# A column mean: one piece of the second-last slab split by rows, fewer loads for the last slab, and a filler matmul taken out

## The chip, the cores and the metric

The kernel runs on one core of a Trainium2 chip. The metric is the device time of one execution in microseconds (us). The engines are called PE (matmuls), PEld (PE's weight loads), DVE (vector), ACT (scalar), POOL and SP (which issues loads and stores here). Loads and stores are carried by 16 DMA engines.

## The reference

```python
def setup_inputs():
    return {"x": np.random.randn(8192, 8192).astype(np.float32)}

def reference(x: np.ndarray) -> np.ndarray:
    return np.mean(x, axis=0)
```

The input is 268 MB of float32; the output is one row of 8192 means.

## The kernel before

**Slabs and pairs.** The 8192 rows are 64 slabs of 128 rows, one row per partition, with all 8192 columns (32 KB a row). The first 62 slabs are read as 31 pairs, each into one of three rotating buffers named `pair` that hold two slabs side by side. Line 96 issues these loads on SP. The first pair comes in two loads, of 2048 columns and the rest; pairs up to the 28th in one load of 16384 columns, and the last three in two loads of 8192. On DVE, line 85 adds the running sum of the pair before to the left half of the new pair, and then the right half to the left half: two additions of 128 x 8192 for each pair. For the last pair the second addition is cut into four of 2048 columns (`parts`, line 107).

**The tail.** The last two slabs share one buffer, `tail`. Its left half is `slab` (slab 62), loaded at line 109 in two loads of 4096 columns. Its right half is `last` (slab 63), loaded at line 112 in nine loads whose widths are in `PIECES`: 2048, 2048, 2048, 1024, 256, 256, 256, 160 and 96 columns. All are issued by SP and served in the order of issue. SP issues a load only when the load eight places ahead of it has landed; the first tail load also waits until DVE has released its buffer.

**Sums over partitions.** PE multiplies by a matrix of ones (128 x 32), which sums the 128 partitions of each column into PSUM. `WIDE` gives four wide ranges of 2048, 2048, 2048 and 1024 columns: `fold_wide` issues four matmuls for a range, each into its own 32 rows of the range's PSUM bank. `NARROW` gives four narrow ranges of 256 columns, one matmul each in `fold_narrow`. A matmul on float32 data is two instructions in the profile. Each column gets three contributions: the running sum (`before`), slab 62 (`slab`) and slab 63 (`last`). For the last 2048 columns, which are wide range 3 and the narrow ranges, DVE adds slab 62 to the running sum first (line 119), so that two contributions are left.

**The order on PE** is the order in which the program is written, each instruction waiting for its data:
1. wide ranges 0, 1 and 2 on `before` and `slab`;
2. `close(0)`: wide range 0 on `last`, then ACT scales it by 1/8192 into `rw`;
3. the filler, line 135: one matmul of 512 columns of `slab` into the bank of narrow range 0, whose result is overwritten (`WARM` counts such matmuls);
4. `close(1)`;
5. wide range 3 and the four narrow ranges on `before`, which wait for DVE's last addition;
6. `close(2)` and `close(3)`;
7. the narrow ranges on `last`, range 3 in two matmuls of 160 and 96 columns. After each range DVE (ranges 0 and 2) or ACT (1 and 3) scales it into `row`.

**Stores.** POOL stores `rw` (line 143) when the third wide range is scaled; SP stores `r3` (line 147) and at the end `row` (line 159).

Of the kernel before, what the change touches and what calls it, by code (L numbers as in the profile page):

```python
# [1 line left out]

# [4 lines left out]

F32 = mybir.dt.float32
ADD = mybir.AluOpType.add
GROUPS = 4  # L10

WIDE = (2048, 2048, 2048, 1024)
NARROW = (256, 256, 256, 256)
PIECES = (2048, 2048, 2048, 1024, 256, 256, 256, 160, 96)
FIRST = 2048
BY_ROW = 3
WARM = 1


@with_exitstack
def kernel(
    ctx: ExitStack,
    tc: tile.TileContext,
    x: bass.AP,
    out: bass.AP,
):
    nc = tc.nc
    P = nc.NUM_PARTITIONS  # L30
    R, C = x.shape
    n_slabs = R // P
    n_pairs = n_slabs // 2 - 1
    N0 = sum(WIDE)
    assert n_slabs % 2 == 0 and n_pairs >= 4 and N0 + sum(NARROW) == sum(PIECES) == C
    inv_r = 1.0 / float(R)

    const_pool = ctx.enter_context(tc.tile_pool(name="const", bufs=1))
    pair_pool = ctx.enter_context(tc.tile_pool(name="pair", bufs=3))
    psum_pool = ctx.enter_context(  # L40
        tc.tile_pool(name="acc", bufs=1, space=bass.MemoryType.PSUM)
    )
    res_pool = ctx.enter_context(tc.tile_pool(name="res", bufs=1))


    ctx.enter_context(tc.manual_schedule())

    ones = const_pool.tile([P, 32], F32)
    nc.gpsimd.memset(ones, 1.0)  # L49

    wide, lo = [], 0
    for n, w in enumerate(WIDE):
        bank = psum_pool.tile([P, w // GROUPS], F32, name=f"wide{n}", tag=f"wide{n}")
        wide.append((lo, w, bank))
        lo += w
    narrow = []
    for n, w in enumerate(NARROW):
        bank = psum_pool.tile([P, 512], F32, name=f"narrow{n}", tag=f"narrow{n}")
        narrow.append((lo, w, 32 * n, bank))
        lo += w  # L60

    def mm(dst, src, **flags):
        nc.tensor.matmul(out=dst, lhsT=ones, rhs=src, skip_group_check=True, **flags)  # L63

    def fold_wide(n, src, **flags):
        lo, w, bank = wide[n]
        q = w // GROUPS
        for g in range(GROUPS):
            a = lo + g * q
            mm(bank[32 * g : 32 * g + 32, :], src[:, a : a + q], **flags)  # L70

    def fold_narrow(n, src, lo, hi, **flags):
        at, _, g, bank = narrow[n]
        mm(bank[g : g + 32, lo - at : hi - at], src[:, lo:hi], **flags)

    def scaled(dst, src, eng):
        if eng == "act":
            nc.scalar.mul(out=dst, in_=src, mul=inv_r)  # L78
        else:
            nc.vector.tensor_scalar(  # L80
                out=dst, in0=src, scalar1=inv_r, scalar2=None, op0=mybir.AluOpType.mult
            )

    def add(dst, a, b):
        nc.vector.tensor_tensor(out=dst, in0=a, in1=b, op=ADD)  # L85

    before = None
    for k in range(n_pairs):  # L90
        pair = pair_pool.tile([P, 2 * C], F32, tag="pair")
        src = x[2 * P * k : 2 * P * (k + 1), :].rearrange("(p j) c -> p (j c)", j=2)
        cut = FIRST if k == 0 else C if k >= n_pairs - BY_ROW else 2 * C
        for lo, hi in ((0, cut), (cut, 2 * C)):
            if lo < hi:
                nc.sync.dma_start(out=pair[:, lo:hi], in_=src[:, lo:hi])  # L96
        if before is not None:
            add(pair[:, 0:C], pair[:, 0:C], before[:, 0:C])
        if k < n_pairs - 1:
            add(pair[:, 0:C], pair[:, 0:C], pair[:, C : 2 * C])  # L100
        before = pair


    tail = pair_pool.tile([P, 2 * C], F32, tag="pair")
    r = (n_slabs - 2) * P
    slab, last = tail[:, 0:C], tail[:, C : 2 * C]
    parts = [(lo, lo + w) for lo, w, _ in wide[:3]] + [(wide[3][0], C)]
    for lo, hi in ((0, C // 2), (C // 2, C)):
        nc.sync.dma_start(out=slab[:, lo:hi], in_=x[r : r + P, lo:hi])  # L109
    lo = 0  # L110
    for w in PIECES:
        nc.sync.dma_start(out=last[:, lo : lo + w], in_=x[r + P : R, lo : lo + w])  # L112
        lo += w


    for lo, hi in parts:
        add(before[:, lo:hi], before[:, lo:hi], before[:, C + lo : C + hi])
    lo, hi = parts[3]
    add(before[:, lo:hi], before[:, lo:hi], slab[:, lo:hi])

    rw = res_pool.tile([P, 3 * 512], F32, name="rw")
    r3 = res_pool.tile([P, WIDE[3] // GROUPS], F32, name="r3")
    row = res_pool.tile([1, C - N0], F32, name="row")

    def close(n):
        fold_wide(n, last, start=False, stop=True)
        scaled(rw[:, n * 512 : (n + 1) * 512] if n < 3 else r3, wide[n][2], "act")

    for n in range(3):
        fold_wide(n, before, start=True, stop=False)  # L130
        fold_wide(n, slab, start=False, stop=False)
    close(0)

    for n in range(WARM):
        mm(narrow[0][3][0:32, :], slab[:, 0:512], start=True, stop=True)
    close(1)
    fold_wide(3, before, start=True, stop=False)
    for n, (lo, w, _, _) in enumerate(narrow):
        fold_narrow(n, before, lo, lo + w, start=True, stop=False)
    for n in range(2, 4):  # L140
        close(n)
    W3 = 3 * GROUPS * 512
    nc.gpsimd.dma_start(  # L143
        out=out[0:W3].rearrange("(n g w) -> g n w", g=GROUPS, w=512),
        in_=rw.rearrange("(g r) (n w) -> g r n w", r=32, w=512)[:, 0],
    )
    nc.sync.dma_start(
        out=out[W3:N0].rearrange("(g w) -> g w", g=GROUPS),
        in_=r3.rearrange("(g r) w -> g r w", r=32)[:, 0],
    )  # L150
    for n, (lo, w, g, bank) in enumerate(narrow):
        if n < 3:
            fold_narrow(n, last, lo, lo + w, start=False, stop=True)
        else:
            cut = C - PIECES[-1]
            fold_narrow(n, last, lo, cut, start=False, stop=True)
            fold_narrow(n, last, cut, C, start=False, stop=True)
        scaled(row[0:1, lo - N0 : lo - N0 + w], bank[g : g + 1, 0:w], "act" if n % 2 else "dve")
    nc.sync.dma_start(out=out[N0:C], in_=row)


# [1 line left out]
_INS = ['x']  # L163
_OUTS = [((8192,), 'float32')]


# [23 lines left out]
```

## Time and profile before

| what | value |
|---|---|
| time, median of 3 runs | 628.18 us (628.05 to 628.44) |
| the profiled execution's own time | 628.08 us |
| its span, first to last instruction | 626.3 us |
| DVE busy | 533.5 us (85%) |
| PE busy | 13.8 us (2%) |
| share of the span of 16 DMA engines, load queue | 99.3% |
| read from memory | 268.44 MB, 429 GB/s over the span |
| chain that ended last | DMA 73%, DVE 25% |
| first matmul, last matmul's start | 608.9 us, 623.4 us |

All times inside an execution are counted from the start of its span. A profile describes one execution; the time around its span (here 1.8 us) is not in it. In the chain that ended last, each step is followed back to what released it. In a table of stretches each row has a stretch's start and end, its length, the busy time of each engine with the number of instructions, the granted TensorE clock, the mean share of the DMA engines that were busy (1.00 is all sixteen), and GB/s. The trace also has a record of each DMA packet with its start, size, duration and queue, but not the engine that carried it.

### The profile page before, as it was taken

What the parts mean: (1) busy time and instruction counts of PE and PEld (TensorE: products, weight loads), DVE (VectorE), ACT (ScalarE), POOL (GpSimd) and SP (SyncE); (2) the same over time, 40 slices, a digit from 0 to 9 for tenths busy, and PEclk for the clock granted to TensorE, in tenths of its full rate; (3) what the DMA queues carried; (4) which work ended last, traced back from release to release, by engine and by line L of the source; (5) the groups of instructions that cost most, each with busy time, mean ns of one, the idle gap of its engine ahead of it and who ended that gap; (6) DMA issues with size and microseconds to landing.
All of it is one profiled execution on the core that took longest, in us unless ns stands there. A gap on an engine that the chain in (4) does not pass through costs nothing.

```text
span 626.3 us, 454 instructions
## 1 busy us (share of the span) xinstructions
PE 13.8 (2%) x108; PEld 4.3 (1%) x108; DVE 533.5 (85%) x67; ACT 4.2 (1%) x7; POOL 1.0 (0%) x6
## 2 busy tenths in 40 slices
PE   0000000000000000000000000000000000000017
PEld 0000000000000000000000000000000000000002
DVE  0538988889888899888898888988889888899995
ACT  0000000000000000000000000000000000000001
POOL 0000000000000000000000000000000000000000
PEclk9999999999999999999999999999999999999999
DMA  9999999999999999999999999999999999999997
GB/s 415 401 456 402 469 402 469 402 469 402 452 419 435 435 419 452 402 469 402 469 402 469 402 469 402 469 402 465 406 465 406 465 406 465 402 431 435 427 422 302
DMA packets 6685, 268.50 MB, mean 429 GB/s; under 512 B 909, under 2 KB 1425, under 8 KB 1562
## 3 DMA queue, kind: packets, MB, share of 16 engines
q1 hardware_dynamic: 6634, 268.45, 99.3%
q0 software_dynamic: 48, 0.02, 0.0%
q8 instruction: 1, 0.02, 0.0%
q14 instruction: 2, 0.02, 0.0%
HBM read 268.44 MB, written 0.03 MB: 429 GB/s over the span
## 4 chain that ended last, share of the span: by engine, by line
DMA 73%; DVE 25%; SPq 0%; PE 0%; issue 0%; ACT 0%; DVEq 0%
DMA pair<-in_x_dram 69%; DVE pair L85 25%; DMA tail<-in_x_dram 5%; SPq L112 0%; PE narrow L63 0%; SPq L96 0%; SPq L109 0%; PE wide L63 0%; ACT row L78 0%; DVEq L85 0%
## 5 line engine op out<-in xcount | busy, mean ns | idle before, releaser
L85 DVE TENSOR_TENSOR pair<-pair 128x8192 f32<-128x8192 f32 (+1 forms) x64 | 530.4, 8292 | 84.9 <-DMA pair<-in_x_dram 83.8
L63 PE MATMUL wide<-pair,ones 128*32 128x512 f32 (+1 forms) x32 | 4.9, 681 | 608.9 <-DVE pair L85 608.9
L63 PE MATMUL wide<-tail,ones 128*32 128x512 f32 (+1 forms) x56 | 7.7, 634 | 0.9 <-DMA tail<-in_x_dram 0.9
L78 ACT ACTIVATE rw<-wide 128x512 f32<-128x512 f32 x3 | 1.8, 597 | 618.4 <-PE wide L63 618.4
L63 PEld LDWEIGHTS wide<-pair,ones 128*32 128x32 f32 x32 | 1.2, 135 | 611.3 <-issue 610.7
L80 DVE TENSOR_SCALAR row<-narrow 1x256 f32<-1x256 f32 x2 | 0.8, 415 | 5.4 <-PE narrow L63 5.4
L63 PE MATMUL narrow<-tail,ones 128*32 128x256 f32 (+3 forms) x12 | 2.5, 385 | 0.0
L85 DVE TENSOR_TENSOR pair<-pair,tail 128x2048 f32<-128x2048 f32 x1 | 2.3, 2291 | 0.0
L63 PEld LDWEIGHTS wide<-tail,ones 128*32 128x32 f32 x56 | 1.7, 118 | 6.4 <-DMA tail<-in_x_dram 3.6
L143 POOL DMA_DIRECT2D out_dram<-rw x1 | 0.7, 695 | 621.7 <-ACT rw L78 621.7
L78 ACT ACT_TABLE_LOAD x1 | 1.3, 1283 | 0.7 <-PEq L174 0.7
L63 PEld LDWEIGHTS narrow<-tail,ones 128*32 128x32 f32 x12 | 1.1, 108 | 1.3 <-issue 0.6
L78 ACT ACTIVATE row<-narrow 1x256 f32<-1x256 f32 x2 | 0.8, 376 | 0.5 <-PE narrow L63 0.5
L63 PE MATMUL narrow<-pair,ones 128*32 128x256 f32 x8 | 0.6, 379 | 0.0
L78 ACT ACTIVATE r<-wide 128x256 f32<-128x256 f32 x1 | 0.4, 383 | 0.2 <-PE wide L63 0.2
L63 PEld LDWEIGHTS narrow<-pair,ones 128*32 128x32 f32 x8 | 0.3, 110 | 0.2
L49 POOL MEMSET ones<- 128x32 f32 x1 | 0.1, 124 | 0.3 <-POOLq L174 0.3
L174 POOL MEMSET const-float32-0.0<- 128x1 f32 x1 | 0.1, 98 | 0.2 <-issue 0.2
L174 POOL MEMSET const-float32-1.0<- 128x1 f32 x1 | 0.1, 98 | 0.0
L174 POOL MEMSET const-bfloat16-1.0<- 128x1 bf16 x1 | 0.1, 98 | 0.0
L174 POOL MEMSET const-uint8-127<- 128x1 uint8 x1 | 0.1, 98 | 0.0
## 6 DMA issues: line engine op xcount, KB each, us to landing
pair<-in_x_dram SPq DMA_DIRECT2D x6, 4096.0 KB, 25.8
pair<-in_x_dram SPq DMA_DIRECT2D x1, 7168.0 KB, 21.2
tail<-in_x_dram SPq DMA_DIRECT2D x2, 2048.0 KB, 21.5
tail<-in_x_dram SPq DMA_DIRECT2D x3, 1024.0 KB, 25.7
pair<-in_x_dram SPq DMA_DIRECT2D x1, 1024.0 KB, 4.7
tail<-in_x_dram SPq DMA_DIRECT2D x1, 512.0 KB, 30.4
pair<-in_x_dram SPq DMA_DIRECT2D x27, 29.9
tail<-in_x_dram SPq DMA_DIRECT2D x3, 128.0 KB, 19.0
```

Of the source, the lines that this page charges most:

```text
L49: nc.gpsimd.memset(ones, 1.0)
L63: nc.tensor.matmul(out=dst, lhsT=ones, rhs=src, skip_group_check=True, **flags)
L78: nc.scalar.mul(out=dst, in_=src, mul=inv_r)
L80: nc.vector.tensor_scalar(out=dst, in0=src, scalar1=inv_r, scalar2=None, op0=mybir.AluOpType.mult)
L85: nc.vector.tensor_tensor(out=dst, in0=a, in1=b, op=ADD)
L143: nc.gpsimd.dma_start(out=out[0:W3].rearrange("(n g w) -> g n w", g=GROUPS, w=512), in_=rw.rearrange("(g r) (n w) -> g r n w", r=32, w=512 ...
L174: nc = _bacc.Bacc("TRN2", target_bir_lowering=False, num_devices=1)
```

## The change

The edit has three parts. The second load of slab 62 ends at column 7680 (`SPLIT`), and the last 512 columns of that slab come in two loads of their own, of rows 0 to 119 (`ROWS`) and rows 120 to 127. The last slab comes in seven loads instead of nine: wide ranges 0 and 1 share one of 4096 columns, narrow ranges 0 and 1 one of 512. The filler matmul is gone, and `close(0)` and `close(1)` stand behind the matmuls of wide range 3 and of the narrow ranges on `before`.

```diff
-PIECES = (2048, 2048, 2048, 1024, 256, 256, 256, 160, 96)
+PIECES = (4096, 2048, 1024, 512, 256, 160, 96)
 FIRST = 2048
 BY_ROW = 3
-WARM = 1
+
+ROWS = 120
+SPLIT = 7680
...
-    for lo, hi in ((0, C // 2), (C // 2, C)):
+    for lo, hi in ((0, C // 2), (C // 2, SPLIT)):
         nc.sync.dma_start(out=slab[:, lo:hi], in_=x[r : r + P, lo:hi])
+    for a, b in ((0, ROWS), (ROWS, P)):
+        nc.sync.dma_start(out=slab[a:b, SPLIT:C], in_=x[r + a : r + b, SPLIT:C])
     lo = 0
     for w in PIECES:
         nc.sync.dma_start(out=last[:, lo : lo + w], in_=x[r + P : R, lo : lo + w])
...
     for n in range(3):
         fold_wide(n, before, start=True, stop=False)
         fold_wide(n, slab, start=False, stop=False)
-    close(0)
-
-    for n in range(WARM):
-        mm(narrow[0][3][0:32, :], slab[:, 0:512], start=True, stop=True)
-    close(1)
     fold_wide(3, before, start=True, stop=False)
     for n, (lo, w, _, _) in enumerate(narrow):
         fold_narrow(n, before, lo, lo + w, start=True, stop=False)
-    for n in range(2, 4):
+    for n in range(4):
         close(n)
```

## The prediction

> **What bounds the kernel now.** I read the page's busy times and slices first. DVE and the loads are both busy nearly all the time, so the question is which of them the end waits for.
>
> ```profile
> span 626.3 us, 454 instructions
> ...
> PE 13.8 (2%) x108; PEld 4.3 (1%) x108; DVE 533.5 (85%) x67; ACT 4.2 (1%) x7; POOL 1.0 (0%) x6
> ...
> DMA  9999999999999999999999999999999999999997
> ...
> q1 hardware_dynamic: 6634, 268.45, 99.3%
> ```
>
> The load queue takes 99.3% of 16 engines' span and moves 268 MB that no edit here makes fewer. Second, the chain of waits from 588 us on, where all of the change lies:
>
> ```profile
> 591.27 30.43 DMA tail<-in_x_dram
> 621.71 0.04 issue
> 621.75 0.64 PE wide L63 x8
> 622.39 1.26 PE narrow L63 x9
> 623.65 0.02 issue
> 623.67 0.38 ACT row L78
> ```
>
> The end follows the last loads; behind them stand only the matmuls of the last columns, one scaling, and the store of `row`. Third, the busy time in short stretches at the end of the loads (columns: PE, PEld, DVE, ACT, POOL, clock, DMA share, GB/s):
>
> ```profile
> 621.80:622.20 0.40, 0.40 (x8) 0.21 (x9) 0.00 (x0) 0.40 (x1) 0.00 (x0) 1.00 0.76 217
> 622.20:622.40 0.20, 0.20 (x5) 0.11 (x2) 0.00 (x0) 0.04 (x1) 0.00 (x0) 1.00 0.07 24
> 622.40:622.60 0.20, 0.20 (x3) 0.14 (x2) 0.00 (x0) 0.14 (x1) 0.06 (x1) 1.00 0.07 22
> 622.60:622.80 0.20, 0.20 (x4) 0.01 (x1) 0.00 (x0) 0.20 (x1) 0.20 (x1) 1.00 0.07 19
> 622.80:623.00 0.20, 0.20 (x3) 0.13 (x2) 0.16 (x1) 0.04 (x1) 0.20 (x1) 1.00 0.00 0
> ```
>
> A share of 0.07 is one engine in 16. So for about 0.55 us a single DMA engine works alone and the kernel waits for it. The trace's packet records say the same: every 128-row load ends in 16 four-byte semaphore packets, one per engine. Their times (us) for the second half of slab 62 and three loads of the last slab (the 15th and 16th of the last two by adding each engine's constant lag; for the last load packets stand at those times):
>
> ```
> load            1st       15th      16th
> slab 62, half 2 611.796   612.211   612.764
> 2048 columns    614.249   614.664   615.217
> 1024 columns    620.403   620.818   621.371
> 96 columns      621.825   622.240   622.793
> ```
>
> The 16th is 0.553 us behind the 15th each time. Up to 409 us no engine is over 0.47 us behind the first; at 413.72 us an 8192-byte packet of the instruction queue appears, and from the next load on one engine that was 0.13 us behind the first is 0.97 behind.
>
> **The change, part by part.** *Price of a load.* On one engine 2048 columns take 614.249 to 616.702 = 2.453 us, 1024 take 1.249 and 256 take 0.345. So 1024 columns cost 1.204 us for an engine's 8 rows, and 0.044 us is the fixed part of a load in a full queue.
>
> *The last slab* goes from nine loads to seven: every engine saves 2 x 0.044 = 0.088 us.
>
> *Slab 62* gets four loads for two. Of the last 512 columns, 128 rows cost each engine 0.602 us now. The trace has no 120-row load. Its 128-row loads give 8 rows to each of 16 engines, and its four-row store of `r3` leaves four semaphore packets on four engines; so I read 120 rows as 8 rows on 15 engines, the 16th spared, and 8 rows as one row on each of eight engines. An engine with 8 rows pays 0.044 for the extra load; one of the eight pays a row besides: 0.602/8 = 0.075 to 0.119 with a whole fixed part. The spared engine pays 0.602 less. With the 0.088:
> - spared engine: -0.690 us
> - 15 others: -0.044, or for eight of them +0.031 to +0.075
>
> If the spared engine is the late one, it ends at 622.793 - 0.690 = 622.10, and the 15th now ends last, at 622.20 to 622.32; I take 622.26, midway, since nothing says in which group it is. The loads end 0.53 us earlier (0.47 to 0.60). If it is not, the late engine ends 0.044 earlier to 0.075 later.
>
> [...]
>
> The uneven loads could also run slower than their bytes, if several engines write into the same place: the farthest row is the 8192-byte packets of the kernel's first load, 0.75 us in the middle for the sixteen that start together and 0.31 us in the running queue. By it the 0.602 us would become 1.44, +0.84 us on every engine. I take nothing, since these rows too stand in a running queue, and keep the 0.84 for the range.
>
> *The queue.* SP issues eleven tail loads before and after. Before, the last one is issued at 615.56 us after a wait for the load eight places ahead, 6 us before its first packet. After, it waits for the 120-row load, which lands near 613. Nothing runs dry. The two stores wait behind the loads on SP as before.
>
> *DVE.* Its last addition needs the columns from 6144 of slab 62, now in three loads. They land by 613.3; DVE is busy until 615.36. That costs nothing; without the 2 us of cover it would delay PE one for one.
>
> *One load for two wide ranges, and the order on PE.* The first range used to close on PE at 615.94, followed by the filler. Both ranges now stand behind the matmuls on the summed pairs, which wait for DVE's last addition. The rows:
>
> ```profile
> 615.39 2.29 DVE L85 TENSOR_TENSOR pair<-pair,tail 128x2048 f32<-128x2048 f32 x1
> ...
> 616.80 1.02 PE L63 MATMUL narrow<-tail,ones 128*32 128x512 f32 x2
> ...
> 618.04 0.64 PE L63 MATMUL wide<-tail,ones 128*32 128x512 f32 x4 [0.22 <-DMA tail<-in_x_dram]
> ```
>
> PE will stand from 615.95 to 617.72 (615.39 + 2.29 and 0.04 to start), 1.77 us, with filler and first range gone from there. A 2048-column range holds PE for 0.86 us (613.37 to 614.23). From 617.72: wide range 3 and four narrow ones on the pairs (0.86) to 618.58, three closes to 621.16, the fourth (0.43) to 621.59, all if their columns are there. The fourth's 1024 columns would land 0.53 earlier than 621.71, at 621.17, so PE has just caught up when the small pieces come. The first two narrow ranges share a load and end near 622.3 instead of 622.80 and 623.03. Then 160 and 96 columns follow the landings. So the 0.53 us passes through the last matmul, ACT and SP.
>
> *The store of `rw`* could become last: its third scaling ends at 622.25 now and it lands at 624.66; 0.2 us earlier at best, 624.45, against 624.9 for `row`. Still covered, by 0.4 us.
>
> *The filler* takes 0.86 us of PE in idle time; removing it saves nothing by itself. Its possible use is the clock. Matmuls of 512 columns took 1061 ns until 611.5 us and 592 from 612.94, so PE runs at half rate until about 3.8 us after its start at 608.9. (The clock column reads 1.00 even then; I go by durations.) Afterwards:
>
> ```profile
> 616.14:619.55 3.41, 3.19 (x30) 1.00 1.00 420
> 619.55:622.97 3.42, 2.71 (x29) 1.00 0.78 280
> 622.97:626.30 3.33, 0.67 (x7) 1.00 0.05 12
> ```
>
> (columns: length, PE busy, clock, DMA share, GB/s). The lowest busy share that later matmuls still ran fast behind is 2.71/3.42 = 79%, and in the last stretch, at 20%, the clock column stays at 1.00 for 2.7 us after the last matmul. After the change the worst 3.41 us around the gap is 48% busy. An idle 1.77 us is shorter than the 2.7 us seen, so I take no loss. [...]
>
> *Sum:* 628.08 (the profiled execution: span 626.3 and 1.8 around it) - 0.53 = 627.55; the median of the runs is 0.10 above that execution, so 627.65.
>
> **Rivals.**
> 1. *The spared engine is not the late one* (or 120 rows are not split so that one is spared). The loads end -0.04 to +0.08 us from now: 628.15 to 628.25, with slow uneven loads up to 629.1. For it: the trace does not name engines, and one in 16 is what blind choice gives.
> 2. *The clock falls in PE's gap: slower.* Place: a fall between 617.7 and 619.6. It decides once PE loses over the 0.5 us or so that it is ahead of the last pieces. Half rate for 3.4 us loses 1.7 us of PE work, so 1.2 us after slack: 627.65 + 1.2 = 628.85, above before. If full rate does not come back, the 4.3 us of work behind 617.72 takes 8.6, the last matmul ends at 626.3 instead of 623.6, and the time is 630.9. For it: 48% is under any share seen at full rate with work after it. Against: the 2.7 us.
> 3. *The uneven loads contend,* +0.84 us on every engine: 628.5, the gain more than eaten.
>
> **How the numbers follow.** [...] Midway, 0.53, is the forecast's chance before the other cases, 0.45 with them. Rival 1: 0.25. Rival 2: 0.16, of it 0.07 with the clock down for good or together with contention. Rival 3: 0.06. The remaining 0.08 is for a gain over 0.2%: it needs a late engine more than twice as late in the timed runs as in the profiled one. 0.2% (1.26 us) is about what a measurement of this kernel can tell from no change: 626.92 to 629.44. Inside it fall the forecast, rivals 1 and 3 and most of 2: 0.85, which I lower to 0.79 for uneven loads dearer than bounded here; faster 0.08, slower 0.13. The range, from the 0.60 us gain with 0.2 us for the spread of the runs to rival 2 at 628.85: 627.3 to 628.9.
>
> **What would show it.** Right: the DMA share falls from near 0.8 to 0 without a stretch at 0.07; the 16th semaphore packet within 0.1 us of the 15th; the last narrow matmul about 0.5 us earlier. Wrong: matmuls of 1061 ns behind 617.7 (rival 2); a lone engine until 622.8 still (rival 1); semaphore times of the 120-row load spread by over 0.3 us more than its neighbours' (rival 3).

## The result, and the profile after

The changed kernel takes 629.06 us (median of 22 runs, 628.33 to 629.94) against 628.05 us for the kernel before (22 runs, 627.62 to 628.44). The ratio is 1.0015, with a 95% interval of 1.0009 to 1.0022. That is 1.0 us slower: inside the 0.2% that were called no change, but clear of the interval, on the other side of the forecast of 627.65 us, and just above the range (627.3 to 628.9). The profiled execution has a span of 627.3 us. In seven of the 22 executions the mean granted clock of PE is 0.997 (629.11 to 629.94, median 629.71); in fourteen it is 1.000, with a median of 628.80, which is 0.75 us above the kernel before, where it is 1.000 in every execution whose clock is on record.

The chain of waits from 588 us on, of the changed kernel:

```profile
593.97 28.81 DMA tail<-in_x_dram
622.77 0.04 issue
622.82 0.64 PE wide L65 x8
623.46 1.16 PE narrow L65 x10
624.61 0.02 issue
624.64 0.38 ACT row L80
```

From the last load on it has the same links as before, each about 1.0 us later: the landing of the 1024 columns at 622.77 instead of 621.71, the last scaling at 624.64 instead of 623.67. Behind the loads nothing grew. The stretches at the end of the loads (columns: start and end, length, PE, PEld, DVE, ACT, POOL, clock, DMA share, GB/s):

```profile
622.40:622.60 0.20, 0.20 (x4) 0.00 (x0) 0.00 (x0) 0.00 (x0) 0.00 (x0) 1.00 1.05 330
622.60:622.80 0.20, 0.05 (x4) 0.00 (x0) 0.00 (x0) 0.08 (x1) 0.00 (x0) 1.00 0.99 286
622.80:623.00 0.20, 0.18 (x4) 0.16 (x8) 0.00 (x0) 0.20 (x1) 0.00 (x0) 1.00 0.52 143
623.00:623.20 0.20, 0.20 (x8) 0.00 (x0) 0.00 (x0) 0.20 (x1) 0.00 (x0) 1.00 0.07 26
623.20:623.40 0.20, 0.20 (x8) 0.00 (x0) 0.00 (x0) 0.12 (x1) 0.00 (x0) 1.00 0.07 22
623.40:623.60 0.20, 0.20 (x6) 0.14 (x4) 0.00 (x0) 0.08 (x1) 0.00 (x0) 1.00 0.07 21
623.60:623.80 0.20, 0.20 (x5) 0.04 (x2) 0.00 (x0) 0.20 (x1) 0.19 (x1) 1.00 0.05 13
```

Two things show. Fifteen engines were busy until 622.9 (the 15th semaphore packet of the last load stands at 622.90 us), where they were done by 622.2 before; and one engine still works alone behind them, now for 0.85 us (the 16th stands at 623.75). So the late engine was not relieved, and the other fifteen were slowed. The profiled executions of the kernels here reach slab 62 up to 0.9 us apart, so for the rest I measure the **tail**: the time from the first engine's semaphore packet of slab 62's first half to the last engine's of the last load. It was 15.86 us before and is 16.55 us after, +0.69; the remaining 0.3 us between the two profiled spans was there before the tail began (that first packet stands at 607.20 us instead of 606.93).

The packets of the late engine in the changed kernel, from the trace's records (start in us, ns, bytes; the sixteen-KB packets of the other engines left out):

```
612.671 245 2048
612.912 202 2048
613.111  95 2048
613.203  85 2048
613.284  84 2048
613.364  84 2048
613.444  84 2048
613.524 120 2048
613.639  11 4
613.646  88 2048
613.731   9 4
```

It carries eight rows of the 120-row load, closes it with a semaphore packet, and carries one of the 8 rows besides. The 120-row load left 15 increments of its semaphore and the 8-row load eight: the split is as the prediction read it, but the engine that was spared is another one, 0.32 us behind the first at that point. It went from slab 62 straight on to the 4096 columns.

The records show the stall too. The 16384-byte packets behind the split took up to 1079 ns, where every such packet took 611 before, and those that were slow began between 611.8 and 614 us, on all sixteen engines. Of the 128 packets of the two loads themselves 99 took the usual 84 to 90 ns, all that began before 612.0 us among them: most of the delay stands in the packets of the load behind the split.

### The profile page after: what moved, and what is told of

Read it like the earlier page. It is cut to its first block, busy times and chain, and to the rows that moved or that the text cites. A ratio compares the mean times of both kernels' runs of the same rounds, so it can differ in the third digit from the quotient of the medians.

```text
span 627.3 us, 451 instructions
## 1 busy us (share of the span) xinstructions
PE 13.0 (2%) x106; PEld 3.8 (1%) x106; DVE 533.5 (85%) x67; ACT 4.2 (1%) x7; POOL 1.0 (0%) x6
## 4 chain that ended last, share of the span: by engine, by line
DMA 77%; DVE 22%; PE 0%; issue 0%; SPq 0%; ACT 0%; DVEq 0%
DMA pair<-in_x_dram 72%; DVE pair L87 22%; DMA tail<-in_x_dram 5%; PE narrow L65 0%; SPq L98 0%; PE wide L65 0%; ACT row L80 0%; DVEq L87 0%
```

## The experiments

**First, which part of the change.** Four kernels, with the row split undone, alone, and at another row, and the order on PE alone.

Row split undone, the rest of the change kept:

```diff
-    for lo, hi in ((0, C // 2), (C // 2, SPLIT)):
+    for lo, hi in ((0, C // 2), (C // 2, C)):
         nc.sync.dma_start(out=slab[:, lo:hi], in_=x[r : r + P, lo:hi])
-    for a, b in ((0, ROWS), (ROWS, P)):
-        nc.sync.dma_start(out=slab[a:b, SPLIT:C], in_=x[r + a : r + b, SPLIT:C])
```

> The changed kernel with slab 62 again in two 128-row loads; seven loads for the last slab, no filler and the new order on PE are kept. If the loss sits in the two loads by rows, the tail (first semaphore packet of slab 62's first half to the last of the last load, 15.86 us before and 16.55 us after) falls to 15.86 - 0.09 = 15.77 us and the time to 0.1 us under the kernel before. If it sits in the order on PE or in the 4096-column load, the time stays about 1 us above before.

Measured: 628.06 us (11 runs) against 628.13 (33 runs); ratio 0.9999 (0.9990 to 1.0007). Tail 15.784 us: 0.076 less than before, for the 0.088 that two loads fewer were to give. The loss is gone.

The row split alone, in the kernel before:

```diff
+ROWS = 120
+SPLIT = 7680
-    for lo, hi in ((0, C // 2), (C // 2, C)):
+    for lo, hi in ((0, C // 2), (C // 2, SPLIT)):
         nc.sync.dma_start(out=slab[:, lo:hi], in_=x[r : r + P, lo:hi])
+    for a, b in ((0, ROWS), (ROWS, P)):
+        nc.sync.dma_start(out=slab[a:b, SPLIT:C], in_=x[r + a : r + b, SPLIT:C])
```

> The kernel before with only the last 512 columns of slab 62 split into 120 and 8 rows; filler, order and nine loads are as before. If the split by rows is the cause, it loses by itself: tail 16.55 + 0.09 = 16.64 us, time about 1 us above before. If the cause needs the large load behind it or the PE order, it stays within 0.2 us of before.

Measured: 629.10 us against 628.13; ratio 1.0014 (1.0005 to 1.0023). Tail 16.664 us. The split loses the whole 1 us by itself.

Only the filler out and the closes moved:

```diff
-    close(0)
-    for n in range(WARM):
-        mm(narrow[0][3][0:32, :], slab[:, 0:512], start=True, stop=True)
-    close(1)
     fold_wide(3, before, start=True, stop=False)
...
-    for n in range(2, 4):
+    for n in range(4):
```

> The kernel before with only the filler taken out and the two closes moved; loads as before. If PE's gap of 1.8 us costs clock, matmuls of 512 columns show 1061 ns again behind 618 us and the time is 0.5 to 1.2 us above before. If not, matmuls stay at 592 ns and the time is that of before within 0.1 us.

Measured: 627.99 us against 628.13; ratio 0.9997 (0.9988 to 1.0006); tail 15.865. With the loads as before, the filler and the order are worth nothing. In this execution PE's gap was only 0.82 us. The changed kernel's own timeline has the gap that was forecast (start, us, engine, line, operation; in brackets the idle time before and what ended it):

```profile
615.30 1.04 PE L65 MATMUL wide<-tail,ones 128*32 128x512 f32 x8
618.01 0.64 PE L65 MATMUL wide<-pair,ones 128*32 128x256 f32 x8 [1.66 <-DVE pair L87]
618.46 0.61 PE L65 MATMUL narrow<-pair,ones 128*32 128x256 f32 x8
619.17 1.07 PE L65 MATMUL wide<-tail,ones 128*32 128x512 f32 x8
```

PE stood idle for 1.66 us, and in this execution the matmuls behind it ran at full rate: eight of 512 columns in 1.07 us, as before.

The split at 112 rows: `ROWS = 112` in the changed kernel.

> The changed kernel with the split at 112 rows, so that 112 and 16 rows can both be spread evenly over 16 engines (7 and 1 rows each). If unevenness between engines is the cause, the loss goes: tail about 15.86 us, no packet of the large load that follows over 0.7 us. If many engines writing into neighbouring partitions is the cause, the 16-row load stalls as the 8-row load does: tail about 16.5 us.

Measured: 628.77 us against 628.13; ratio 1.0012 (1.0003 to 1.0021); tail 16.451; packets of the following load up to 871 ns. Each of its two loads left sixteen semaphore packets, one per engine, and still the loss stays. That speaks against unevenness, and I read it as crowding by the small load, which was wrong, as the next four show.

**Second, the loads by themselves.** Each kernel is the kernel before with one more load behind slab 62, of 512 columns into a spare tile that nothing reads:

```diff
+    spare = res_pool.tile([P, 512], F32, name="spare")
+    nc.sync.dma_start(out=spare[120:128, :], in_=x[r + 120 : r + P, 0:512])
```

with the tile's rows 120:128, 0:32:4, 112:128 and 0:120 in turn, and as many rows of x.

> The kernel before plus one load whose data is not used, behind slab 62: 8 rows of 512 columns into partitions 120 to 127 of a spare tile. If an 8-row load into neighbouring partitions stalls the engines, its 2048-byte packets take over 84 ns, the 8192-byte packets behind it over 0.31 us, and the tail grows by about 0.5 us over 15.86. If such a load costs its bytes and one fixed part, the tail grows by 0.08 to 0.12 us at most.

> As the 8-row load of the kernel before it, but into partitions 0, 4, 8 to 28, so that no two engines write into the same group of four partitions. If crowding of neighbouring partitions stalls, this one does not: packets at 84 ns, tail at most 0.12 us longer. If leaving the engines uneven stalls, this one stalls as much as the other: about 0.5 us.

> The kernel before plus an unused load of 16 rows of 512 columns into partitions 112 to 127: even for all 16 engines, crowded in four groups of partitions. Crowding: stall, tail about 0.5 us longer. Unevenness: no stall, tail 0.08 to 0.12 us longer.

> The kernel before plus an unused load of 120 rows of 512 columns into partitions 0 to 119. By bytes the 15 engines that carry it lose 0.65 us and one loses none. If the 120-row load itself stalls, the tail grows by over 1.0 us and the packets behind it are slow; if not, by 0.65 us, or by less where the spared engine is the late one.

Measured, one execution each (628.05, 628.55, 627.91 and 629.37 us against 628.22): tails 15.957, 15.951, 15.952 and 17.216 us. Loads of 8 or 16 rows cost 0.09 to 0.10 us, a row and a fixed part, in all three layouts. The 120-row load costs 1.356 us, 0.65 of it by its bytes and 0.7 beyond. So the 8-row load of 2-KB rows is innocent, and the 120-row load stalls the queue without it. Three microseconds around it, in the stretches of four kernels (before; with 16 rows; with 120 rows; the changed kernel):

```profile
611.00:614.00 3.00, 3.00 (x24) 0.87 (x20) 3.00 (x2) 0.00 (x0) 0.00 (x0) 1.00 0.95 401
```
```profile
611.00:614.00 3.00, 3.00 (x28) 0.90 (x24) 3.00 (x2) 0.00 (x0) 0.00 (x0) 1.00 0.96 404
```
```profile
611.00:614.00 3.00, 3.00 (x24) 0.86 (x20) 3.00 (x2) 0.00 (x0) 0.00 (x0) 1.00 0.98 347
```
```profile
611.00:614.00 3.00, 3.00 (x24) 0.80 (x20) 3.00 (x3) 0.00 (x0) 0.00 (x0) 1.00 1.03 341
```

The last two numbers are the DMA share and GB/s. The engines look fully busy in all four, at a share near 1, while the bytes fall from some 400 to some 345 GB/s (the kernels that do not stall have 396 to 431 in this stretch): the same bytes take longer packets. So a share near 1 does not show a full rate: 0.98 stood here with 347 GB/s, 0.95 with 401.

**Third, the suspected cost made large.** The whole second half of slab 62, 4096 columns, in two loads by rows, in the kernel before:

```diff
+    nc.sync.dma_start(out=slab[:, 0 : C // 2], in_=x[r : r + P, 0 : C // 2])
+    for a, b, s in ((0, 64, 1), (64, P, 1)):
+        nc.sync.dma_start(out=slab[a:b:s, C // 2 : C], in_=x[r + a : r + b : s, C // 2 : C])
```

The other two have ((0, 120, 1), (120, P, 1)), and ((0, P - 1, 2), (1, P, 2)) for even and odd rows.

> The kernel before with the whole second half of slab 62 (4096 columns, eight times the piece of the change) loaded as 120 rows and 8 rows. If every byte of a 120-row load is slow because engines share places to write, the loss grows with the bytes: 8 x 0.6 = about 4.8 us. If the split only disturbs the engines once, it stays near 0.7 us plus the 0.6 us that one more 16-KB row costs eight engines.

> The kernel before with the second half of slab 62 loaded as rows 0 to 63 and rows 64 to 127: every engine has 4 rows of each. If a load into 64 neighbouring partitions has only half of the ways into the buffer, its 2.4 us become 4.8 for each half: 4.8 us in all. If row splits cost only a disturbance, about 0.7 us; if only uneven counts cost, 0.04 us.

> As the split in halves, but even rows and odd rows. The engines' shares then lie over all partitions, though not the share that each engine has in a 128-row load. If the number of different partition groups written at once is what counts, the loss lies between 0 and that of the halves, less than half of it. If any assignment other than that of 128 rows costs, it is as large as for the halves.

Measured, one execution each, against 628.02 us for the kernel before: 636.05 us (tail 23.908), 635.45 us (tail 21.958) and 628.17 us (tail 15.830). Six microseconds in which these loads run, first 120 + 8 rows, then halves, then even and odd rows:

```profile
608.00:614.00 6.00, 5.04 (x32) 1.46 (x36) 6.00 (x4) 0.00 (x0) 0.00 (x0) 1.00 1.01 218
```
```profile
608.00:614.00 6.00, 5.14 (x28) 1.33 (x32) 6.00 (x4) 0.00 (x0) 0.00 (x0) 1.00 1.02 213
```
```profile
608.00:614.00 6.00, 5.04 (x32) 1.45 (x36) 6.00 (x4) 0.00 (x0) 0.00 (x0) 1.00 0.96 411
```

Rows 0 to 63 and then 64 to 127 run at half rate (213 GB/s, against 419 in the same stretch of the kernel before); the same number of rows taken two apart runs at full rate (411), with every 16384-byte packet at 611 ns as in a 128-row load. The number of loads and of rows is the same; what differs is which partitions are written at one time, and with them which rows of `x` are read at one time. So the cost lies in which rows a load takes, and it goes on for as long as the load does. That it is the writing and not the reading is not shown by a run: no kernel here pairs neighbouring rows of `x` of that number with partitions two apart. The halves' rate is what the expectation's half of the ways into the buffer would give; such ways themselves no run shows. Nor does a run show by what means a load of 120 or 112 rows is slow: which rows an engine carries stands in no record, so for these the reason stays open.

Halves and 120 rows lost more in all than I expected at 4.8 us, 6.1 and 8.0 us of tail. Behind the halves the 8192-byte packets of the next loads stay slow for some 2 us, up to 680 ns instead of 309. With 120 rows it is worse: from 616 to 620 us, where the 8-row load of 16-KB rows and the next load run, the stretch has 135 GB/s, with 8192-byte packets of up to 1572 ns.

**Fourth, why one engine is late.** ACT issues the loads of the first 21 pairs, in the kernel with the row split undone:

```diff
+ACT_LOADS = 21
-                nc.sync.dma_start(out=pair[:, lo:hi], in_=src[:, lo:hi])
+                (nc.scalar if k < ACT_LOADS else nc.sync).dma_start(out=pair[:, lo:hi], in_=src[:, lo:hi])
```

> The changed kernel without the row split, and with the first 21 pairs' loads issued by ACT, the rest by SP, so that neither issues more than about half. If the instruction packet at 413.7 us belongs to SP's long program and is what makes one DMA engine late, the packet is gone or later, the last engine ends within 0.5 us of the first, and the time is 0.5 us below the kernel without the row split: about 627.5. If the late engine has another cause, 0.97 us of lag and 628.1 us stay.

Measured: 628.03 us against 628.02; ratio 1.0003 (0.9994 to 1.0012). A miss: the instruction packet came at 420.73 us, and the last engine was 1.05 us behind the first. The same with 11 pairs, and a kernel with 24 small memsets at the start of DVE's program:

```diff
+    pad = const_pool.tile([P, 8], F32, name="pad")
+    for n in range(24):
+        nc.vector.memset(pad, 0.0)
```

> As the kernel with loads issued by ACT, but ACT issues only the first 11 pairs and SP the rest. If the packet belongs to the program of the engine that issues the loads and comes after some 23 of them, SP now reaches that only in the tail: no packet near 414 us, and no engine 0.97 us late before 600 us. If it belongs to DVE, it stays near 414 to 421 us.

> The changed kernel without the row split, with 24 tiny memsets of a spare tile put at the start of DVE's program, done long before the first data lands. If the instruction packet that makes one DMA engine late belongs to DVE's program, it comes earlier by the time in which DVE now issues 24 instructions, at least 100 us, and the engine is late from then on. If it belongs to SP's program, it stays at 413.7 us, within 1 us.

Measured, one execution each (628.20 and 629.24 us). With 11 pairs from ACT the packet stays at 413.79 us, although SP has issued only half as many loads by then. With the memsets it comes at 259.05 us, and the last engine is 1.24 us behind the first from the next load on instead of 0.49. The step is 154.7 us, eight pairs at 19.33 us; DVE issues three instructions for a pair (two additions and a wait), so 24 instructions are eight pairs. The other traces agree: in all sixteen the packet comes some 4 us after the start of DVE's 63rd recorded instruction (413.72 and 409.58 us in the kernel before), while SP has 9 to 45 behind it and ACT 3 to 43. That also explains the 420.73 us above, where DVE reached its 63rd instruction 7 us later. So I read the packet as a fetch of DVE's own program: it comes at a fixed place in that program, and the engine that carries it is late for the rest of the kernel (still 0.97 us behind the first in the last load of the kernel before): with 309 ns of its own the packet costs that engine about 0.84 us (from 0.13 to 0.97 us behind the first). The memset kernel's tail is 16.254 us, longer than the 15.784 of the same kernel without memsets; its one execution ran most 16384-byte packets at 614 instead of 611 ns, for which no run gives a reason.

No kernel here beats both. The one with the row split undone has the shortest tail but for the 11 pairs from ACT (15.747 us), and neither difference is one that the times can tell.

## Why the prediction was wrong, by its steps

- **The bound was right.** The end follows the last loads, and within them one late engine. In the kernels with the row split undone, alone and at 112 rows, and with 120 rows of the wide piece, the time moved as the tail did, within the spread of the runs. It did not in two others: the halves lost 1.3 us more than their tail, after PE's clock had fallen, and the 21 pairs from ACT had a tail 0.7 us longer (its engines were already up to 1.8 us apart where the tail is counted from) at the same median time.
- **"If the spared engine is the late one"** was the step on which the sign hung, and it failed: the late engine carried nine of the split's rows. The gain of 0.53 us rested on it. The chance of 0.53 was the middle between blind choice, one in 16, and certainty, and no row of the profile stood behind it. No run shows the certainty either: the engine that the packet had made late carried eight rows of the 120-row load and one of the 8. Rival 1 was the case, with its sign: a lone engine until 623.75 us.
- **"I take nothing, and keep the 0.84 for the range"** failed too. The row that I took the 0.84 from shows packets that start together, and is no measure of this (and 0.602 x 0.751/0.309 is 1.46, not 1.44). The 120-row load stalls in a running queue, where I had put the cost at nothing; rival 3's sign came too, with semaphore packets of that load 1.53 us apart, against 0.97 for the loads ahead. The late engine's sum, worked out with the packets above: slab 62 ends 6.530 us after the tail's start instead of 5.831, +0.70. One row and a semaphore packet are 0.09 of it, the extra load's fixed part 0.04, which leaves 0.57 of stall. In the 4096 columns behind it stalls for 0.08 more, and two loads fewer give 0.09 back. That is the +0.69 of the tail. The bound of 0.84 held, but as a thing apart: rivals 1 and 3 came together (629.1 in the prediction's text for rival 1 with slow loads), and the range was cut at 628.9.
- **Loads of 8 rows** cost 0.09 to 0.10 us, inside the 0.075 to 0.119 that was worked out, and the fixed part is as forecast: -0.076 us for two loads fewer.
- **The order on PE, the filler and DVE** were right with the loads as before, by the run with the order alone (all 11 executions at a clock of 1.000). In the profiled execution of the changed kernel the clock stayed as well: the stretch from 616.14 to 619.55 is 1.67/3.41 = 49% busy, where 48% was worked out as the worst, and full rate held (eight matmuls of 512 columns in 1.07 us). But "I take no loss" does not hold for all executions. The seven at a mean clock of 0.997 have a median 0.91 us above the fourteen at 1.000, and 0.3% of 627 us is what some 3 to 4 us at half rate would take away (an estimate: 0.003 x 627 / 0.5 = 3.8). So a fall of the clock as in rival 2 came in about a third of them, on top of the rest. The split alone, with filler and old order, kept 1.000 in all 11 executions; so did the kernel with the split undone and the new order, whose stretch is 2.36/3.41 = 69% busy. Two of 11 executions at 112 rows and two of 11 with 21 pairs from ACT have 0.997 too. Where the clock fell in these executions, no kept profile shows. Nor does a run record the 3.4 us at half rate that give rival 2 its 628.85 and the range its upper end: the two falls that a record has during PE's work, with the halves and with 120 wide rows, stay at half for 6.83 us.
- **The instruction packet** was named as the start of the lateness; that it is DVE's was not, and SP's was my first guess.

## What to carry to other kernels

Before a load is cut by rows, ask which rows and partitions it takes at one time: here 64 neighbouring rows ran at half rate (213 GB/s), the same count two rows apart at full rate (411), and a load of 120 rows stalled the whole queue (347 GB/s instead of 401, with 0.7 us lost beyond its bytes). A plan that shifts work off one slow resource needs a row that says which resource it is; a share of 0.07 says that one engine is late, and not that it is the one which the edit spares. A load of 16 or 32 KB behind a full queue is cheap here (0.09 to 0.10 us). Filler matmuls bought nothing with the loads as before (11 executions of 11 kept the clock without them); with the row split seven of 22 without them did not, and 11 of 11 with them did. And one profiled execution is not all of them: compare the granted clock of every run before saying that it held.

## What the runs showed of the hardware beyond that

The clock fell with longer gaps, of 3.81 us with the halves and 6.17 us with 120 wide rows. In the kernel with the halves, PE waits 3.81 us for slab 62 and the clock falls soon after the wait:

```profile
619.71 1.06 PE L63 MATMUL wide<-tail,ones 128*32 128x512 f32 x8 [3.81 <-DMA tail<-in_x_dram]
621.80 1.93 PE L63 MATMUL wide<-tail,ones 128*32 128x512 f32 x8 [1.02 <-DMA tail<-in_x_dram]
```

The first eight matmuls behind the gap still take 1.06 us, the next eight 1.93, half rate: the clock record falls at 620.85 us, and the 3.41 us before that hold 1.06 us of matmuls, 31% busy. The profiled execution of the changed kernel, at 49% in a stretch of that length, kept the clock. So a fall as in rival 2 did come. Whether the busy share of such a stretch decides it, and at which share, two executions do not show, and others of the changed kernel lost clock. In the kernels with the halves and with 120 wide rows the record stays at half for 6.83 us, twice the 3.4 us that rival 2 was priced at. And 24 idle-time instructions on DVE are not free here: they move a fetch, from 413.7 to 259.05 us, and with it a lateness of about 0.8 us, from one load to another.
